# One block of a hybrid encoder: GLA's output and Hyena's second inverse transform computed by rows, Hyena's gates turned by VectorE, the last query projection by rows

## The chip, the cores and the metric

The kernel runs on one core of one Trainium2 chip. The metric is the device time of one execution in microseconds; the time of a kernel is the median of several runs. A core has TensorE (PE in the profile, with its weight loads shown apart as PEld), VectorE (DVE), ScalarE (ACT), GpSimd (POOL) and SyncE (SP), each with its own instruction queue, worked off in order; here SP issues the loads of weights and inputs, and POOL the transfers that pass a result through DRAM and back.

## The reference, cut to what matters

The kernel computes one block on 256 rows of width 2048 in f32: four mixers side by side, cross attention over 256 memory rows, a gated MLP, and a last norm.

```python
h = rms_norm(x, norm_g[l, 0])
q, k, v, g, lr, u_f, u_h, u_s = jnp.split(h @ w_in[l], split_at, axis=-1)
y_a = gla_mixer(q, k, v, g, lr, ...)                       # 512 wide
y_b = rms_norm(fnet_mixer(u_f), grp_norm_g[l, 0])          # 512 wide
y_c = rms_norm(hyena_mixer(u_h, hy_conv_w[l], filt, ...), grp_norm_g[l, 1])
y_d = rms_norm(shortconv_mixer(u_s, sc_conv_w[l]), grp_norm_g[l, 2])
x = x + jnp.concatenate([y_a, y_b, y_c, y_d], axis=-1) @ w_out[l]
x = x + cross_attention(rms_norm(x, norm_g[l, 1]), mem_n, w_q, w_kv, w_o)
x = x + swiglu(rms_norm(x, norm_g[l, 2]), w_gate_up, w_down)

# gla_mixer: 4 heads, chunks of 64 rows, forward and backward
o = rms_norm(o_intra + o_inter, norm_g) * silu(g)          # norm over the 128 of a head
# hyena_mixer: u after a convolution of three taps is split into v, x1, x2
z = x1 * long_conv(v, filt[0], skip[0])
return x2 * long_conv(z, filt[1], skip[1])                 # long_conv: rfft, product, irfft
```

## The kernel before, in words

**Layouts.** A tile *by columns* has 128 features on the partitions and the 256 rows along the free axis; a tile *by rows* has 128 rows on the partitions and up to 512 features along the free axis. A matmul reads its left operand with the contracted features on the partitions, so every result that feeds the next matrix must end by columns.

**Splitting.** f32 products are made from two fp32r parts: a high part (a cast on ACT) and a low part (a subtraction on DVE). An activation lies in a slot of 512 columns, high then low. The weights come as slabs of 1 MB; each half slab (eight blocks of 128 x 128) is cast by L102 on ACT and subtracted by L103 on DVE, a few halves ahead of its use (`Stream._half`, `Stream.take`).

**The two forms of a large product.** `gemm` (L296, L297) takes a weight block as the left operand and gives columns: per block one matmul of 512 and one of 256 columns. `gemm_rows` (L345 to L347) takes the activation as the left operand and four weight blocks as the moving one and gives rows: three matmuls of 512 columns for each half of the rows. `ROWS` lists which of the 4032 weight blocks are used by rows; it sets the place of the split tiles. What comes by rows and is needed by columns is transposed in blocks of 32 x 32 by DVE and written to DRAM (`store_turned`, L386 and L388) and read back (`load_turned`, L393), the features in a permuted order that the host puts into the weight matrix that follows (`turned`).

**Background work.** The mixers and the attention heads are Python generators. `Background.poll` is called after each weight block or pair of matmuls and lets a generator step when its due time in counted TensorE time is past and the counted DVE work owed is under 0.9 us. `yield` with a number sets the next due time; `drain` runs a generator to its end at once. `keep_place` pins instructions to their place in their engine's order.

**The part around the change**, in order of time in the profile:

- 193 to 265 us: `gemm` of Hyena's 12 column blocks. `Hyena.feed` convolves each by three taps (`conv3`); blocks 0 to 3 (v) and 4 to 7 (x1) are turned to rows by TensorE transposes (L1064) one block later, x1 is copied by ACT (L1073); blocks 8 to 11 (x2) stay by columns.
- Beside it and after it `Hyena.convs` runs: a transform (L1103), the product with the filter, an inverse transform by rows (L1103), times x1, a transform again, the product, and the second inverse transform by columns in plain f32 (L1277: 16 matmuls, each of which shows as two records), times x2. `group_norm` then sums squares by matmuls with a column of ones (L244), spreads the scale by two matmuls with a matrix of ones (L280), scales and splits into `act[16:20]`.
- 265 to 342 us: projections by rows of GLA's v, q and k, and of FNet. Then everything pending is drained, and Hyena's memory is given to GLA.
- 342 to 426 us: three projections by rows (two for the short convolution, one for GLA's gate). Beside them FNet and GLA: the gates' logarithms and running sums, the scores of each chunk (L1397, L1398), the gain of each chunk's state (`gain`, L1420, a contraction over 64 rows), the state recursion on DVE, and the output by columns (L1444, L1447), 423 to 433 us.
- GLA's output is normed over a head's 128 features, which lie on the partitions: eight matmuls with a column of ones (L244, 16 records), `rstd_end` with two matmuls of ones per head (L280), the product with the norm, then with the gate, which had been through DRAM to come by columns, and the split into `act[4:8]`.
- 426 to 453 us: the last projection of the short convolution, by columns.
- From 453 us: `out_proj` takes the 16 slots in four parts of four: Hyena, FNet, GLA, short convolution. Before each part after the first, `ready` drains the generator that fills it and loads 512 columns of x into the freed tiles through SP.
- 542 to 640 us: the query projections of the four heads; the first three by rows and through DRAM, the last one (610 to 640 us) by `gemm`, merged and split by `put` without leaving the chip. `scores` runs the heads one after another; what is left of them is drained before the last quarter of the next projection's first two column blocks (686.65 us).

## Time and profile before

| | |
|---|---|
| median of 3 runs | 1469.69 us (1469.57 to 1469.91) |
| the profiled execution | 1470.08 us |
| its span, first to last instruction | 1468.3 us |
| TensorE busy | 1458.3 us |
| VectorE, ScalarE, GpSimd busy | 921.9, 740.4, 192.1 us |
| granted TensorE clock, mean | 0.998 |

The chain rows read "start, duration, engine, tile, line", a duration being what the step adds to the chain. In timeline rows a matmul's duration runs to its modelled end and overlaps the next one, so distances between starts are what counts there. A row of waits is "who, line <- for whom: total, times, longest". In a row of windows each engine has its busy time and its instructions.

### The profile page before, as it was taken

What the parts mean: (1) busy time and instruction counts of PE and PEld (TensorE: products, weight loads), DVE (VectorE), ACT (ScalarE), POOL (GpSimd) and SP (SyncE); (2) the same over time, 40 slices, a digit from 0 to 9 for tenths busy, and PEclk for the clock granted to TensorE, in tenths of its full rate; (3) what the DMA queues carried; (4) which work ended last, traced back from release to release, by engine and by line L of the source; (5) the groups of instructions that cost most, each with busy time, mean ns of one, the idle gap of its engine ahead of it and who ended that gap; (6) DMA issues with size and microseconds to landing.
All of it is one profiled execution on the core that took longest, in us unless ns stands there. A gap on an engine that the chain in (4) does not pass through costs nothing.

```text
span 1468.3 us, 18130 instructions
## 1 busy us (share of the span) xinstructions
PE 1458.3 (99%) x6792; PEld 1214.9 (83%) x6792; DVE 921.9 (63%) x1320; ACT 740.4 (50%) x1060; POOL 192.1 (13%) x256
## 2 busy tenths in 40 slices
PE   9999999999999999999999999999999999999997
PEld 7888888888888888888888888888888888888886
DVE  6677868777778676675665555455555456444445
ACT  6566655446656455564554444444444445434344
POOL 0000000022121233520511110111110011000000
PEclk9999999999999999999999999999999999999999
DMA  9887554456556788954866666666666666555554
GB/s 348 298 282 249 207 193 168 152 202 201 198 183 211 236 265 263 267 162 151 266 219 221 225 216 198 220 226 229 214 211 216 218 211 223 198 185 190 198 200 144
DMA packets 59240, 318.07 MB, mean 217 GB/s; under 512 B 9197, under 2 KB 10894, under 8 KB 27536
## 3 DMA queue, kind: packets, MB, share of 16 engines
q1 hardware_dynamic: 46208, 281.11, 55.6%
q0 software_dynamic: 12512, 35.14, 8.9%
q8 instruction: 53, 0.87, 0.2%
q10 hardware_dynamic: 432, 0.66, 0.1%
q14 instruction: 35, 0.29, 0.1%
HBM read 297.48 MB, written 19.40 MB: 216 GB/s over the span
## 4 chain that ended last, share of the span: by engine, by line
PE 96%; ACT 1%; DVE 1%; DMA 1%; issue 0%; SPq 0%; ACTq 0%
PE pg L345 27%; PE pg L346 27%; PE pg L347 27%; PE pg L296 5%; PE pg L297 3%; PE pm L347 1%; PE pm L346 1%; PE pm L345 1%; PE pm L1103 1%; PE pm L860 1%; PE pm L831 1%; DMA raw<-in_W 0%; DVE wl L103 0%; DMA tmp<-in_cfn 0%; ACT wh L102 0%
## 5 line engine op out<-in xcount | busy, mean ns | idle before, releaser
L103 DVE TENSOR_TENSOR wl<-raw,wh 128x1024 fp32r<-128x1024 f32 (+1 forms) x503 | 611.5, 1217 | 479.3 <-ACT wh L102 478.8
L102 ACT CAST wh<-raw 128x1024 fp32r<-128x1024 f32 (+1 forms) x503 | 523.7, 1043 | 591.3 <-PE pg L347 515.3
L345 PE MATMUL pg<-wh,act 128*128 128x512 f32 (+1 forms) x1618 | 631.8, 391 | 0.4 <-ACT wh L102 0.4
L346 PE MATMUL pg<-wl,act 128*128 128x512 f32 (+1 forms) x1618 | 629.9, 389 | 0.8 <-DVE wl L103 0.8
L347 PE MATMUL pg<-wh,act 128*128 128x512 f32 (+1 forms) x1618 | 630.0, 389 | 0.0
L345 PEld LDWEIGHTS pg<-wh,act 128*128 128x128 f32 x1618 | 303.8, 188 | 64.9 <-issue 1.2
L346 PEld LDWEIGHTS pg<-wl,act 128*128 128x128 f32 x1618 | 303.9, 188 | 63.8 <-DVE wl L103 1.8
L347 PEld LDWEIGHTS pg<-wh,act 128*128 128x128 f32 x1618 | 303.8, 188 | 63.4
L296 PE MATMUL pg<-act,wh 128*128 128x512 f32 x320 | 113.0, 395 | 0.0
L297 PE MATMUL pg<-act,wl 128*128 128x256 f32 x320 | 89.8, 280 | 0.0
L296 PEld LDWEIGHTS pg<-act,wh 128*128 128x128 f32 x320 | 60.2, 188 | 12.6
L388 POOL DMA_DIRECT2D hidden<-u x22 | 16.7, 762 | 377.8 <-DVE u L386 377.8
L297 PEld LDWEIGHTS pg<-act,wl 128*128 128x128 f32 x320 | 60.2, 188 | 0.2
L347 PE MATMUL pg<-wh,f 128*128 128x512 f32 x120 | 46.8, 390 | 0.0
L345 PE MATMUL pg<-wh,f 128*128 128x512 f32 x120 | 46.8, 390 | 0.0
L346 PE MATMUL pg<-wl,f 128*128 128x512 f32 x120 | 46.7, 389 | 0.0
L393 POOL DMA_DIRECT2D tmp<-hidden x44 | 38.8, 888 | 47.3 <-DMA hidden<-u 34.6
L388 POOL DMA_DIRECT2D features<-tmp x32 | 22.7, 716 | 99.3 <-DVE tmp L386 99.3
L347 PEld LDWEIGHTS pg<-wh,f 128*128 128x128 f32 x120 | 22.5, 188 | 4.8
L346 PEld LDWEIGHTS pg<-wl,f 128*128 128x128 f32 x120 | 22.5, 188 | 4.6
L345 PEld LDWEIGHTS pg<-wh,f 128*128 128x128 f32 x120 | 22.5, 188 | 4.5
L393 POOL DMA_DIRECT2D ar<-features x24 | 21.1, 887 | 20.3 <-DMA features<-tmp 16.9
(308 smaller groups left out, 1120.6 us busy)
## 6 DMA issues: line engine op xcount, KB each, us to landing
raw<-in_W SPq DMA_DIRECT2D x246, 1024.0 KB, 5.0
raw<-in_W SPq DMA_DIRECT2D x11, 512.0 KB, 7.2
hidden<-u POOLq DMA_DIRECT2D x22, 256.0 KB, 3.5
tmp<-hidden POOLq DMA_DIRECT2D x44, 128.0 KB, 4.6
features<-tmp POOLq DMA_DIRECT2D x32, 128.0 KB, 2.3
ar<-features POOLq DMA_DIRECT2D x24, 128.0 KB, 6.3
k<-in_mem SPq DMA_DIRECT2D x8, 256.0 KB, 7.9
keys<-k POOLq DMA_DIRECT2D x8, 256.0 KB, 7.0
```

Source lines behind the costliest of these rows:

```text
L102: nc.scalar.copy(wh[:, a:b], r[:, a:b])
L103: nc.vector.tensor_tensor(out=wl[:, a:b], in0=r[:, a:b], in1=wh[:, a:b].bitcast(F32), op=ALU.subtract)
L296: self.nc.tensor.matmul(p[:, :], wh, slot[:, :], start=start, stop=False)
L297: self.nc.tensor.matmul(p[:, 0:R], wl, slot[:, 0:R], start=False, stop=stop)
L345: self.nc.tensor.matmul(p, hi, wh, start=start, stop=False)
L346: self.nc.tensor.matmul(p, hi, wl, start=False, stop=False)
L347: self.nc.tensor.matmul(p, lo, wh, start=False, stop=stop)
L388: self.nc.gpsimd.dma_start(to[r], u.rearrange("p (k c) -> p k c", c=P))
L393: self.nc.gpsimd.dma_start(t.rearrange("p (g t) -> p g t", t=32), src)
L831: nc.tensor.matmul(p[:, :], q[d][:, r * P:(r + 1) * P], kt[d][:, :], start=d == 0, stop=False)
L860: nc.tensor.matmul(p[:, 0:R], v[m][:, s], pt[m][:, c:c + R], start=m == 0 and v is vh and c == 0, stop=m == 1 and v is vl)
L1103: self.b.nc.tensor.matmul(p, a, b, start=start and n == 0, stop=stop and n == 2)
```

## The change

GLA's output matmuls swap their operands: the left one is now the scores (128 columns) or the query of one chunk (64 columns, one chunk to partitions 0 to 63 of the result and the other to 64 to 127), the moving one v or the state. The result comes by rows; the norm's sums come from ACT's accumulated squares and its scale from `rstd_cols` (DVE alone), and norm and gate are one DVE instruction per head and half of the rows. The gate stays by rows and no longer passes through DRAM; the gated output does, and is split when it has arrived and the last projection of the mixers is done. The two gains that use different halves of the partitions are issued in turns.

Hyena's second inverse transform takes the form of the first (`back`). x1 and x2 are transposed by DVE and sent through DRAM by two loads each (`turn`). The result is normed by rows, stored and loaded into `res[1]`, and split from there by `long_conv`, a background generator after GLA's start. `out_proj` takes the short convolution third and GLA fourth. The last query projection is done like the other three.

```diff
-ROWS = ((0, 512), (704, 1088), (1152, 1600), (1664, NBLK))
+ROWS = ((0, 512), (704, 1088), (1152, NBLK))
...
+                g_long = self.bg.add(self.long_conv())
...
-                for r, j in halves:
-                    t = self.tmp()
-                    nc.scalar.activation(t, ps[r][:, j:j + R], AF.Silu)
-                    self.store_turned(self.gf, j // P, r, self.tmp(), t)
-                for k in range(4):
-                    self.load_turned(gl.gate[k], self.gf, k)
+                for g, p in zip(gl.gate, ps):
+                    nc.scalar.activation(g, p, AF.Silu)
+                gl.gated = True
...
+                self.bg.drain(g_long)
                 self.gemm("w_in", [US + i * P for i in range(4)], h, ev_s)
                 gl.done = True
-                return self.out_proj(lambda n: self.bg.drain((g_fn, g_gla, g_sc)[n]))
+                return self.out_proj(lambda n: self.bg.drain((g_fn, g_sc, g_gla)[n]))
+
+    def long_conv(self):
+        nat = lambda x: x.rearrange("p (i two) -> p two i", two=2)
+        yield 14
+        for k in range(4):
+            x = self.res[1][:, k, :].rearrange("p (two i) -> p two i", two=2)
+            hi, lo = (nat(self.act[16 + k][:, c:c + R]) for c in (0, R))
+            g = self.gvec(V_GRP + 4, k)
+            mark = self.mark()
+            self.nc.scalar.activation(hi, x, AF.Copy, scale=g)
+            self.stt(lo, x, g, hi.bitcast(F32), ALU.mult, ALU.subtract)
+            self.keep_place(mark)
+            yield SOON
...
-                for c in ((0,), (2, 3), (1,))[n - 1]:
+                for c in ((0,), (1,), (2, 3))[n - 1]:
...
-        return self.gemm_rows("w_out", [0, 512], self.mix, parts=[range(k, k + 4) for k in (8, 4, 0, 12)], before=ready)
+        return self.gemm_rows("w_out", [0, 512], self.mix, parts=[range(k, k + 4) for k in (8, 4, 12, 0)], before=ready)
...
-            self.gemm("w_xq", [1536 + i * P for i in range(4)], h2, lambda i, p: last.append(self.merge(p)))
-            self.bg.add(scores(3), go=True)
+            queries(3, self.gemm_rows("w_xq", [1536], h2)[0])
...
+    def turn(self, y, d, to, j):
+        u = b.tmp()
+        b.bg.dve(R, 2)
+        for par, x in enumerate(y.rearrange("p (f b two) -> p two b f", b=4, two=2)[:, i] for i in range(2)):
+            nc.vector.transpose(u[:, par * P:(par + 1) * P].rearrange("p (b f) -> p b f", b=4), x)
+        nc.gpsimd.dma_start(d.rearrange("(t p) c -> p t c", p=P), u.rearrange("p (t c) -> p t c", c=P))
+        for par in range(2):
+            nc.gpsimd.dma_start(to[:, par, j * P:(j + 1) * P]..., d[par * P:(par + 1) * P]...)
...
-        for j in range(4):
-            for par in range(2):
-                for cs in range(2):
-                    nc.tensor.matmul(p[:, par * P:(par + 1) * P], self.y[cs][par][:, s], self.table(cs, par), ...)
-        yield from b.group_norm(out, 1, b.act[16:20])
+        yield from self.back(ps)
+        for par, x in enumerate(rows):
+            b.tt(x, ps[par], self.x2[:, par, :], ALU.mult)
+            nc.scalar.activation(ps[par], x, AF.Square, accum_out=col[:, par:par + 1])
+            yield SOON
+        yield
+        y = b.rstd_cols(col, 512)
+        for par, x in enumerate(rows):
+            nc.scalar.activation(x, x, AF.Copy, scale=y[:, par:par + 1])
+            yield
+            for j in range(0, 512, R):
+                b.store_turned(b.hf, j // P, par, b.tmp(), x[:, j:j + R])
+        for k in range(4):
+            b.load_turned(b.res[1][:, k, :], b.hf, k)
...
+        def gains(*cs):
+            us = [b.bank() for _ in cs]
+            for h in range(4):
+                for u, c in zip(us, cs):
+                    d = slice((c % 2) * 64, (c % 2) * 64 + 64)
+                    nc.tensor.matmul(u[:, h * P:(h + 1) * P], self.kr[d, c // 2, h, :], self.v[c // 2][d, h * P:(h + 1) * P], ...)
...
+        for r in range(2):
+            p = b.bank()
+            for h, hv in enumerate(heads):
+                nc.tensor.matmul(p[:, hv], self.s[r][:, h, :], self.v[r][:, hv], start=True, stop=False)
+                for i in range(2):
+                    d = slice(i * 64, i * 64 + 64)
+                    nc.tensor.matmul(p[d, hv], qs[:, h, r * P + i * 64:r * P + i * 64 + 64], st[:, 2 * r + i, h, :], start=False, stop=True)
+            for h, hv in enumerate(heads):
+                nc.scalar.activation(self.q[:, h, 0:P], p[:, hv], AF.Square, accum_out=col[:, 4 * r + h:4 * r + h + 1])
+            nc.scalar.copy(self.o[r], p)
+            yield
+        yield
+        y = b.rstd_cols(col, P)
+        while not self.gated:
+            yield
+        for r in range(2):
+            for h, hv in enumerate(heads):
+                b.stt(self.o[r][:, hv], self.o[r][:, hv], y[:, 4 * r + h:4 * r + h + 1], self.gate[r][:, hv], ALU.mult, ALU.mult)
+            ...
+                b.store_turned(b.gf, j // P, r, b.tmp(), self.o[r][:, j:j + R])
+        yield from b.arrive(b.gf, 0, b.tmp, lambda h, t: b.split_scaled(slots[h], t, b.gvec(V_GLA, 0)), 13.0, lambda: self.done)
```

122 lines of the change are left out of this document (44 added, 78 removed).

## The prediction

> **What bounds the kernel now.** I read the page's busy times first, then its chain of waits by engine, then what TensorE itself waited for.
>
> ```profile
> PE 1458.3 (99%) x6792; PEld 1214.9 (83%) x6792; DVE 921.9 (63%) x1320; ACT 740.4 (50%) x1060; POOL 192.1 (13%) x256
> ...
> PE 96%; ACT 1%; DVE 1%; DMA 1%; issue 0%; SPq 0%; ACTq 0%
> ```
> ```profile
> PE pg L346 <- DVE wl L103: 0.8, 3, 0.3
> ```
>
> TensorE is busy for 99% of the span, 96% of the chain is its instructions, and what it waits for longest once its work has begun is the low part of a weight split, 0.8 us in all. So a matmul that goes is worth its whole step in the chain, one that comes costs it, and work of DVE, ACT, POOL and SP is free until it makes a weight split or a slot late. I price the matmuls from the chain, whose durations are distances between starts, and then look for the places where the cover is thin.
>
> ```profile
> 230.38 0.23 PE pm L1064 x2
> ...
> 236.16 0.23 PE pm L1064 x2
> ...
> 242.17 0.37 PE pm L1064 x2
> ...
> 248.10 0.36 PE pm L1064 x2
> ...
> 271.08 1.37 PE pm L1103 x6
> ...
> 310.73 1.78 PE pm L1277 x16
> ...
> 315.27 1.78 PE pm L1277 x16
> ...
> 325.93 0.34 PE pm L244 x4
> ...
> 334.55 0.24 PE pm L280 x2
> ```
> ```profile
> 266.27 1.86 PE pm L469 x32
> ...
> 389.07 0.23 PE pg L347
> 389.29 0.30 PE pm L1397
> ...
> 389.60 0.11 PE pm L1397
> ...
> 390.38 0.43 PE pg L345
> ...
> 405.76 3.09 PE pm L1420 x32
> ...
> 424.04 0.39 PE pm L1447 x4
> 424.43 0.28 PE pm L1444 x2
> ...
> 438.45 1.68 PE pm L244 x16
> 440.13 0.34 PE pg L296
> ...
> 452.38 0.47 PE pm L280 x4
> ...
> 462.74 0.47 PE pm L280 x4
> ```
>
> **The change part by part: TensorE.**
>
> *x1's transposes.* The last four L1064 rows are x1's eight transposes; they go: 0.23 + 0.23 + 0.37 + 0.36 = 1.19 us gained.
>
> *Second inverse transform.* Two L1277 rows go (3.56 us), two sets of six matmuls like the L1103 row come (2 x 1.37 = 2.74): 0.82 gained.
>
> *Hyena's norm.* L244 (0.34) and L280 (0.24) go. A first large matmul behind an L244 takes 0.34 (row at 440.13) instead of 0.23, so 0.11 goes too: 0.69 gained.
>
> *GLA's norm.* L244 1.68, again 0.11 behind it, L280 twice 0.47: 2.73 gained.
>
> *The gains in turns.* The model is L1397 and L1398, two matmuls on different halves of the partitions issued in turns: the row 389.29 to the row 390.38 is 1.09 us for 16 records of each kind but only eight steps of 0.11, as the other half runs abreast. The gains' 32 records (3.09 us today) become 16 such steps, eight more than there: 1.09 + 8 x 0.11 = 1.97. Gained: 1.12.
>
> *GLA's output.* The part that can cost. Today one head and half of the rows take 0.28 (L1444) + 0.39 (L1447, four records of 64 columns) = 0.67; eight of them make 5.36. In the new form the first product keeps its shape (0.22, two records at L1397's 0.11), and the two chunks become two matmuls of 128 columns on 64 columns of the array each. Two things of that shape are not in the trace. Whether the two run abreast: the nearest row is L469, on a quarter of the array's columns, 32 records of 256 columns in 1.86 us; at L1277's 0.11 us for 128 columns they would take 7 us one behind the other, so four run abreast. I take two abreast: 0.22 for the pair, against 0.44 in series. And what changing the shape costs: the first L1397 takes 0.30 instead of 0.11, and the large matmul behind the last L1398 takes 0.43 instead of 0.23, so about 0.20 for each change. The new loop alternates full and half shape for every head and half of the rows, 16 changes. With both: 8 x (0.22 + 0.20 + 0.22 + 0.20) = 6.72, a loss of 1.36. Free changes would give 8 x 0.44 = 3.52, a gain of 1.84; paid changes with the pair in series 8.48, a loss of 3.12. I take the middle one: both its halves have a row.
> The Trainium skill, page "TensorEngine Tiling (Array Packing)", section "Key Properties", states that a change of tiling mode, as opposed to a change of tile, drains the engine, and that different tiles work independently. By it alternating at this grain speaks against the change; the 0.20 us at both ends of L1397 agree, and that section gives no price.
>
> *Last query projection by rows.*
>
> ```profile
> 254.67 0.39 PE L296 MATMUL pg<-act,wh 128*128 128x512 f32 x1
> ...
> 264.38 0.39 PE L296 MATMUL pg<-act,wh 128*128 128x512 f32 x1
> ```
> ```profile
> 290.17 0.39 PE L345 MATMUL pg<-wh,act 128*128 128x512 f32 x1
> ...
> 297.65 0.39 PE L345 MATMUL pg<-wh,act 128*128 128x512 f32 x1
> ```
>
> By columns 28 blocks take 264.38 - 254.67 = 9.71, that is 0.347 each; by rows eleven steps of three matmuls take 297.65 - 290.17 = 7.48, 0.68 a step, and two steps do four blocks, so 0.340 a block. 64 blocks: 0.43 gained.
>
> Sum on TensorE: 1.19 + 0.82 + 0.69 + 2.73 + 1.12 + 0.43 - 1.36 = **5.6 us gained**.
>
> **The change part by part: what must stay hidden.**
>
> ```profile
> 230.00:260.00 30.00, 30.00 (x176) 26.28 (x175) 29.09 (x45) 17.61 (x28) 0.00 (x0) 1.00 0.49 165
> ```
> ```profile
> L198 DVE TENSOR_TENSOR k<-k,k 128x512 f32<-128x512 f32 x24 | 16.4, 685 | 0.3
> ...
> L202 DVE SCALAR_TENSOR_TENSOR rc<-rc 128x2 f32<-128x2 f32 x36 | 5.8, 160 | 1.0
> ...
> L202 DVE SCALAR_TENSOR_TENSOR act<-tmp,vec,act 128x256 fp32r<-128x256 f32 x8 | 3.8, 479 | 0.0
> ...
> L386 DVE STREAM_TRANSPOSE tmp<-tmp 128x256 f32<-128x256 f32 x8 | 3.2, 426 | 2.2 <-ACT tmp L593 2.2
> ```
> ```profile
> 318.20 0.99 POOL L1315 MEMSET gs<- 128x512 f32 x2 [122.63 <-DVE res L198]
> ```
> ```profile
> 368.98 0.22 ACT L1384 ACTIVATE gref<-gref 128x16 f32<-128x16 f32 x1 [4.52 <-DVE gref L1362]
> ```
> ```profile
> 376.13 0.50 PE L346 MATMUL pg<-wl,act 128*128 128x512 f32 x1 [0.32 <-DVE wl L103]
> ```
>
> *Turning x1 and x2.* Sixteen half transposes on DVE, two for each of eight column blocks; a whole one of this size takes 0.43, so each pair between 0.43 and 0.86: 3.4 to 6.9 us, in a stretch where DVE is already busy for 29.09 of 30 us (the fourth pair of numbers in the window's row). They are not throttled, but Hyena's transforms beside them are: their generator steps only when little DVE work is owed. So it is the transforms that move, by about as much. Today the last Hyena matmul is at 334.55, and the drain comes with the end of FNet's projection at 342; the new chain's last matmul is the second inverse transform, today at 315.27, with the splits of its operands some 320 (an estimate: four subtractions of 0.685 on DVE). Cost 0 on TensorE. The 24 DMAs on POOL fall into the 122.63 us that it idles before 318. If that cover went, the wait is for x1, first needed behind the L1103 row at 271.08, over 20 us after the transpose of its last block at 248.10.
>
> *Hyena's result through DRAM.* Four stores and four loads on POOL, behind GLA's loads; the slots are first read by `out_proj`, four projections later. Cost 0.
>
> *`long_conv`.* This is the thin place. ACT stands 4.52 us in front of L1384 until DVE has finished GLA's running sums, its weight casts stand behind it, and the row at 376.13 shows the one stall of TensorE away from the start. Four ACT scalings and four DVE instructions of 0.48 (the second L202 row), 1.9 us on DVE, come due 14 us after 342, just ahead of it. In front of L1384 each microsecond of them is one of TensorE; in the gaps of DVE before it they are free. So 0 to 1.9, and I take 0.8: some find gaps, as the generators share the budget of owed work.
>
> *GLA's gate and output.* The gate's eight DMAs go, the output's eight come, all on POOL, which stands idle there; the split waits for the end of the mixers' last projection as before. In fourth place in `out_proj` it has a part more than now. Cost 0.
>
> *Short convolution third instead of fourth.*
>
> ```profile
> 475.75 0.24 PE pm L280 x2
> ```
> ```profile
> 479.16 1.42 DVE L198 TENSOR_TENSOR act<-res,act 128x256 fp32r<-128x256 f32 x4
> ```
>
> The third part began right behind that L280, at 476.0; the convolution's first slot was ready at 479.16 + 0.36 = 479.5. Unmoved, it would hold TensorE for 3.5 us. But GLA's norm and splits, which stood before it on DVE and in the owed budget, are mostly gone from this stretch. From 0 to 3.5 us; I take 0.4. The loads of x change places with it on SP, that of column 1 now a part earlier, the others a part later; their first reader comes after the whole product: 0.
>
> *Head 3.* Its queries now take the way through DRAM, due 18 us of counted time after the projection's end; its scores also wait for head 2 and for the values, as now.
>
> ```profile
> 682.67 1.41 PE pm L860 x12
> ```
> ```profile
> 686.65 0.39 PE L345 MATMUL pg<-wh,act 128*128 128x512 f32 x1
> ```
>
> Its last matmuls end at 684.1, and the part that needs its slots starts at 686.65. 0 to 2 us; I take 0.1, since the wait for the queries ends before the one for the values. On POOL the four stores and four loads stand in front of the last loads of values; with five buffers in use these are asked for early.
>
> **Sum.** 5.6 gained, 0.8 + 0.4 + 0.1 lost: 4.3 us. The profiled execution took 1470.08, so 1465.8; the median of the runs is 0.39 below that execution, so **1465.4 us**.
>
> **The rivals.**
>
> *Changes of shape are free at this grain.* For it: L1447 behind L1444 shows no gap, though there the shape is the same. Against: both ends of L1397 and L1420. Another 3.2 us gained: 1462.2.
>
> *The half-array pair runs in series.* For it: the two have one head's accumulator in one bank. Against: L469's four quarters share a bank too. 1.76 lost: 1467.2.
>
> *The short convolution is late in its new place*, at nearly today's pace: about 3.1 beyond my 0.4, 1468.5.
>
> *Slower: Hyena's end falls behind the drain at 342.* If the turned x1 and x2 push the transforms so far that the second inverse transform and all behind it are drained there, DVE gets, ahead of GLA's sums: four subtractions and two products of 512 columns (six by the first DVE row's 0.685: 4.1), the norm's twelve small ones (by 0.16: 1.9), four transposes (by 0.426: 1.7) and `long_conv`'s 1.9: 9.6 us, in a stretch where a late microsecond is one of TensorE. 9.6 - 5.6 = 4.0 slower than the median, 1473.7. It decides only when the chain slips by over 22 us (320 to 342); the transposes explain at most 6.9. Less of a slip brings part of it, and up to 8.5 us of stall the kernel is not over 0.2% slower.
>
> **How the numbers follow.** 0.2% (2.9 us) is about what a measurement of this kernel can tell from no change; faster is below 1466.75. My forecast 0.56, with its own range 1463.7 to 1466.7; free changes 0.09 (faster); pair in series 0.09 and late convolution 0.09 (both within); Hyena behind the drain 0.08 (slower). What I have not seen gets 0.09: 0.05 on the faster side, 0.04 on the slower. Faster 0.70, within 0.18, slower 0.12. The range 1462.0 to 1470.0 takes in free changes at its lower end, the pair in series and the late convolution, and a stall of 1.9 for `long_conv` on top of either; it leaves out the slow cases.
>
> **What the changed profile would show.** TensorE still at 99%, no L244 and L280 for Hyena and GLA. The gains near 2.0 us. GLA's output as eight groups with starts 0.8 us apart, near 0.65 if changes are free or 1.06 if the pair is in series. TensorE's waits for weight splits around 365 to 380 at 0.5 to 2 us; a DVE or ACT wait of a first matmul on the third part of `out_proj` would be the late convolution, and an L1103 behind 335 the slow case. The forecast is wrong if the waits of TensorE grow by over 3 us, wherever that is.

## The result and the profile after

The changed kernel takes 1473.46 us, the median of 13 runs (1470.85 to 1475.69), beside 1470.02 us for the kernel before: a ratio of 1.0022 (95% interval 1.0015 to 1.0029). It is slower by 0.22%; 1465.4 was predicted, with a range that ended at 1470.0. The profiled execution took 1471.93 us with a span of 1470.1, so it is one of the quicker ones.

The page's busy times and the shares of the chain by engine, after:

```profile
PE 1455.8 (99%) x6702; PEld 1207.3 (82%) x6702; DVE 924.8 (63%) x1325; ACT 737.4 (50%) x1051; POOL 222.7 (15%) x296
...
PE 96%; DVE 1%; ACT 1%; DMA 1%; issue 0%; SPq 0%; ACTq 0%; DVEq 0%
```

TensorE works 2.5 us less than before (1455.8 against 1458.3), yet the span is 1.8 us longer: the idle time of TensorE rose by 4.3 us. (0.84 us of the longer span lies ahead of the change, in the loads of the start.) Its waits (who, line <- for whom: total, times, longest), after:

```profile
PE pg L345 <- ACT act L206: 2.8, 1, 2.8
PE pm L431 <- DVE eps L432: 1.1, 1, 1.1
PE pg L346 <- DVE wl L103: 0.9, 3, 0.4
PE pm L1529 <- DVE fal L198: 0.9, 1, 0.9
PE pm L1529 <- ACT fah L214: 0.8, 1, 0.8
```

Before, the longest of these was the second kind, at the start, and the next 0.8 in all. Three are new: one of 2.8 us on a slot, and two on FNet's operand (`fah`, `fal`). The chain of after at the places whose rows the prediction priced (start, duration, engine, tile, line):

```profile
323.94 1.37 PE pm L1120 x6
328.07 1.37 PE pm L1120 x6
...
418.15 1.98 PE pm L1446 x32
...
432.59 0.37 PE pm L1474 x4
432.96 0.42 PE pm L1471 x2
433.38 0.37 PE pm L1474 x4
```

The second inverse transform is two rows of 1.37, the gains take 1.98, and GLA's output repeats every 0.79 us (432.59 to 433.38). So the work came out as it was priced. What went wrong shows when the time is cut at the first matmul of each projection. This table is worked out from both traces (durations before; differences in the profiled executions of the other kernels; e1 to e14 are told below):

```
stage                        before   after     e1     e2     e4     e6    e13    e14
Hyena's projection            71.57   -1.25  -1.25  -1.24  -1.24  +0.00  -1.24  -1.24
the next three                77.43   -1.54  -1.54  -1.54  -1.54  -0.00  -1.53  -1.54
w_in 4640 (FNet, GLA)         30.05   +0.31  +5.87  +2.75  -3.10  -0.05  -1.04  -3.44
w_in 1024                     29.05   -2.39  -2.39  -2.39  -0.90  +0.00  -2.40  -0.90
w_in 3616 by columns          27.46   +1.27  +1.28  +1.27  +1.28  -0.00  +1.27  -0.80
out_proj, first part          12.31   -1.08  +0.06  -1.07  -1.05  +0.00  -1.04  -1.04
  second part (to 3rd's start) 11.17  +4.07  +0.00  +0.61  +4.07  +1.66  +4.06  +0.61
  third part                  10.91   +1.73  +0.01  +0.36  +1.65  +0.10  +3.00  +0.28
last query projection and xo  76.65   -0.18  -0.12  -0.11  -0.15  +0.05  -0.10  -0.18
```

Every other stage differs by less than 0.05 us, but for the first 24 us, where the loads of the start vary by up to 2.0 us. Two stretches took back what the rest gained: the turn from the second to the third part of `out_proj` (+5.8), and the projection under which FNet's and GLA's chains run, which varies from +5.87 in e1 to +0.31 in the changed kernel although the instructions are the same up to there. TensorE's timeline at the third part, after:

```profile
473.32 0.28 PE L280 MATMUL pm<-dgh,ones 128*128 128x256 f32 x1
473.59 0.39 PE L280 MATMUL pm<-dgl,ones 128*128 128x256 f32 x1
476.76 0.58 PE L345 MATMUL pg<-wh,act 128*128 128x512 f32 x1 [2.79 <-ACT act L206]
477.14 0.63 PE L346 MATMUL pg<-wl,act 128*128 128x512 f32 x1
477.57 0.63 PE L345 MATMUL pg<-wh,act 128*128 128x512 f32 x1
478.00 0.63 PE L346 MATMUL pg<-wl,act 128*128 128x512 f32 x1
478.42 1.06 PE L347 MATMUL pg<-wh,act 128*128 128x512 f32 x2
479.27 0.63 PE L345 MATMUL pg<-wh,act 128*128 128x512 f32 x1
479.70 0.63 PE L346 MATMUL pg<-wl,act 128*128 128x512 f32 x1
480.13 0.55 PE L347 MATMUL pg<-wh,act 128*128 128x512 f32 x1
480.52 0.40 PE L345 MATMUL pg<-wh,act 128*128 128x512 f32 x1
```

The short convolution's first slot comes 2.79 us late, and then the matmuls start 0.427 us apart instead of 0.227 until 480.5: half speed for 3.7 us, some 1.7 us more; that is the +1.73 of the third part's row in the table. The page's clock row (9 in each of 40 slices) doesn't show it. What stood in front of the slot, on DVE and on ACT, after:

```profile
474.65 1.23 DVE L103 TENSOR_TENSOR wl<-raw,wh 128x1024 fp32r<-128x1024 f32 x1 [1.11 <-ACT wh L102]
475.79 1.27 DVE L202 SCALAR_TENSOR_TENSOR res<-res,vec,rs 128x256 f32<-128x256 f32 x3
```
```profile
474.52 0.37 ACT L283 COPY rs<-pm 128x256 f32<-128x256 f32 x1
476.31 1.20 ACT L206 CAST act<-res 128x256 fp32r<-128x256 f32 x3 [1.41 <-DVE res L202]
```

The norm's broadcast, a weight split that happens to be in between, the product and the cast follow one another, with TensorE behind them all. In the 20 us before (454 to 474), DVE is busy for 13.4 us and ACT for 9.6: they had room. So I take it that the convolution's generator came late; e1 tests this.

### The profile page after: what moved, and what is told of

The parts are those of the page before. It is cut to its first block, busy times and chain, and to the rows that moved or that the text cites. A ratio compares the mean times of both kernels' runs of the same rounds, so it can differ in the third digit from the quotient of the medians.

```text
span 1470.1 us, 18016 instructions
## 1 busy us (share of the span) xinstructions
PE 1455.8 (99%) x6702; PEld 1207.3 (82%) x6702; DVE 924.8 (63%) x1325; ACT 737.4 (50%) x1051; POOL 222.7 (15%) x296
## 4 chain that ended last, share of the span: by engine, by line
PE 96%; DVE 1%; ACT 1%; DMA 1%; issue 0%; SPq 0%; ACTq 0%; DVEq 0%
PE pg L345 27%; PE pg L346 27%; PE pg L347 27%; PE pg L296 4%; PE pg L297 2%; PE pm L345 1%; PE pm L346 1%; PE pm L347 1%; PE pm L1120 1%; PE pm L868 1%; DMA raw<-in_W 1%; DVE wl L103 1%; PE pm L839 1%; DMA tmp<-in_cfn 0%; ACT wh L102 0%
## 5 line engine op out<-in xcount | busy, mean ns | idle before, releaser
L345 PE MATMUL pg<-wh,act 128*128 128x512 f32 (+1 forms) x1650 | 645.6, 391 | 2.9 <-ACT act L206 2.8
L346 PE MATMUL pg<-wl,act 128*128 128x512 f32 (+1 forms) x1650 | 643.8, 390 | 0.9 <-DVE wl L103 0.9
L347 PE MATMUL pg<-wh,act 128*128 128x512 f32 (+1 forms) x1650 | 643.5, 390 | 0.0
L345 PEld LDWEIGHTS pg<-wh,act 128*128 128x128 f32 x1650 | 310.6, 188 | 69.4 <-ACT act L206 3.0
L346 PEld LDWEIGHTS pg<-wl,act 128*128 128x128 f32 x1650 | 310.5, 188 | 65.1 <-DVE wl L103 2.0
L347 PEld LDWEIGHTS pg<-wh,act 128*128 128x128 f32 x1650 | 310.5, 188 | 64.6
L296 PE MATMUL pg<-act,wh 128*128 128x512 f32 x256 | 89.9, 394 | 0.0
L297 PE MATMUL pg<-act,wl 128*128 128x256 f32 x256 | 71.7, 280 | 0.0
L296 PEld LDWEIGHTS pg<-act,wh 128*128 128x128 f32 x256 | 48.1, 188 | 10.6 <-issue 0.3
L297 PEld LDWEIGHTS pg<-act,wl 128*128 128x128 f32 x256 | 48.1, 188 | 0.2
```

Source lines behind the costliest of these rows:

```text
L296: self.nc.tensor.matmul(p[:, :], wh, slot[:, :], start=start, stop=False)
L297: self.nc.tensor.matmul(p[:, 0:R], wl, slot[:, 0:R], start=False, stop=stop)
L345: self.nc.tensor.matmul(p, hi, wh, start=start, stop=False)
L346: self.nc.tensor.matmul(p, hi, wl, start=False, stop=False)
L347: self.nc.tensor.matmul(p, lo, wh, start=False, stop=stop)
```

## The experiments

Theory A: the loss is the short convolution's slot, late in its new third place, and the half-speed steps that its wait sets off. Rival B: FNet's waits and GLA's changes of shape. Rival C: the slow steps have nothing to do with the wait. All medians stand beside 1470.2 to 1470.6 for the kernel before on the same chip.

**e1: the convolution's generator first in the queue.**

```diff
-                g_sc = self.bg.add(short_conv(u0), go=True)
+                g_sc = self.bg.add(short_conv(u0), first=0, go=True)
```

> The changed kernel with one word moved: the short convolution's generator is put at the head of the background queue, so that it steps before FNet's and GLA's when little work is owed. The order of the parts of `out_proj` stays as in the changed kernel. Theory A (the loss is the short convolution's slot being late at the third part, 2.79 us of wait on the split's cast, and the matmuls behind it that step 0.427 us instead of 0.227, some 1.8 us): the wait and the slow steps go together, GLA's generator is pushed back and its first slot may come up to 1 us late in the fourth part; 1473.5 - 4.6 + 0 to 1.0 = 1468.9 to 1469.9 us. Rival B (the loss is GLA's output on arrays of changing shape and FNet's waits at 374 us): the time stays within 1 us of 1473.5. Rival C (the slow steps are a thing of that place or of the chip, not of the wait): the wait goes, but eight or so matmuls still step 0.427 us near 477 us; 1470.5 or above.

1468.07 us (ratio 0.9985, 0.9975 to 0.9996), 5.4 less than the changed kernel. The wait and the slow steps at the third part are gone (+0.00 and +0.01 in the table), so A holds for this place. But the 12 runs fall into two groups, six at 1465.0 to 1466.4 and six at 1469.7 to 1472.1, and the profiled one (1471.77) shows why, at FNet (TensorE's timeline, e1):

```profile
376.40 0.73 PE L1529 MATMUL pm<-fah,fch 128*128 128x512 f32 x1 [2.11 <-ACT fah L214]
377.78 0.80 PE L1529 MATMUL pm<-fal,fch 128*128 128x512 f32 x1 [0.65 <-DVE fal L198]
378.37 0.63 PE L1529 MATMUL pm<-fah,fcl 128*128 128x512 f32 x1
...
380.08 0.63 PE L345 MATMUL pg<-wh,act 128*128 128x512 f32 x1
```

The waits that were 0.8 and 0.9 in the changed kernel's profile are 2.1 and 0.65 here, with eleven steps at half speed behind them. So a part of rival B holds too, and half speed is not tied to `out_proj`, which speaks against C. The granted clock of the runs fits this: 0.998 or 0.999 in all six quick ones, 0.996 or 0.997 in five of the six others.

**e2: the order of `out_proj` undone.**

```diff
-                return self.out_proj(lambda n: self.bg.drain((g_fn, g_sc, g_gla)[n]))
+                return self.out_proj(lambda n: self.bg.drain((g_fn, g_gla, g_sc)[n]))
...
-                for c in ((0,), (1,), (2, 3))[n - 1]:
+                for c in ((0,), (2, 3), (1,))[n - 1]:
...
-        parts=[range(k, k + 4) for k in (8, 4, 12, 0)]
+        parts=[range(k, k + 4) for k in (8, 4, 0, 12)]
```

> The changed kernel with the order of `out_proj` undone alone: GLA third, the short convolution fourth, and the loads of x as before. Theory A: the short convolution has a part more (10.9 us) and is in time; GLA's arrival is due 13 us of counted time after its store and comes to be drained at the third part, so its first scaled cast and subtraction (0.53 and 0.48 us by the changed kernel's rows) stand in front of TensorE: a wait of about 1 us there, and none of 2.8. 1473.5 - 4.6 + 1.0 = 1469.9 us, 1469 to 1471. Rival B: within 1 us of 1473.5. Rival D (GLA is what is late, whatever the order: what the third part waits for is DVE's and ACT's work, not the place in the queue): a wait of 2 us or more on GLA's slot, and 1473 to 1475 us.

1468.70 us (0.9987, 0.9979 to 0.9996): 4.8 less, a little more than A expects, and the wait for GLA's slot that I expected in its place is not there. D falls. FNet's two waits are in this profile too, 1.7 and 0.9 us, with seven steps at half speed behind them.

**e3: four changes of shape instead of sixteen.**

```diff
             for h, hv in enumerate(heads):
-                nc.tensor.matmul(p[:, hv], self.s[r][:, h, :], self.v[r][:, hv], start=True, stop=False)
+                nc.tensor.matmul(p[:, hv], self.s[r][:, h, :], self.v[r][:, hv], start=h == 0, stop=False)
+            for h, hv in enumerate(heads):
                 for i in range(2):
```

> The changed kernel, with GLA's output in two passes for each half of the rows: the four products of all 128 columns first, then the eight of 64 columns, so four changes of shape instead of sixteen; the number of matmuls and the result are the same. If a change of shape costs its 0.16 to 0.20 us each (6.08 us measured for the output against 8 x 0.44 = 3.52 with free changes), the output takes 3.52 + 4 x 0.16 = 4.2 us and the kernel 1.9 us less: 1471.6 us. If the time lies in something else (the two matmuls of a pair do not quite run abreast, or the sums into the same bank wait for each other), the output stays near 6 us and the time near 1473.5. The late short convolution is untouched: its wait of about 2.8 us stays.

1469.90 us (0.9999, 0.9990 to 1.0008), 3.6 less. The chain, e3:

```profile
431.84 0.89 PE pm L1471 x8
432.73 1.02 PE pm L1475 x16
```

Half of the output takes 1.91 us instead of 2.95 (432.37 to 435.32 in the changed kernel). The stage (`w_in` 3616) is 2.08 us shorter than in the changed kernel: 0.17 for each of the 12 changes that went. The other 1.5 us of the medians is not the shapes: in this profile FNet's first wait is 0.2 instead of 0.8.

**e4: FNet's second product due 2 us later.**

```diff
-                yield 4.0 if g else LAG
+                yield 6.0 if g else LAG
```

> The changed kernel with FNet's second product due 6.0 instead of 4.0 us of counted time behind the split of its operand, so that the cast (ACT) and the subtraction (DVE), which stand behind GLA's sums at 374 us, are done when TensorE comes to them. If the two waits at 374.40 and 375.78 (0.77 and 0.88 us) are a price of their own: they go, and the time is 1.7 us less, 1471.8 us. If the place only moves them (GLA's chain holds ACT as long, and what is behind is late instead): the waits turn up at the next product or at a weight split, and the time stays within 0.5 us of 1473.5. The late short convolution stays as it is.

1470.00 us (0.9999, 0.9991 to 1.0008), 3.5 less; ten of the 11 runs lie between 1469.0 and 1471.4. FNet's waits are gone, the convolution's (2.7) is still there. The two stages under FNet are 1.9 us shorter than in the changed kernel's quick profile; that the median gained more would fit longer waits in its slower runs, of which there is no trace.

**e5: stalls put into the kernel before.**

```diff
+        def stall(hd):
+            def done(k):
+                (start_x if hd == 3 else rows.append)(k)
+                if k in (3, 11):
+                    s = h[k + 1][:, 0:R]
+                    p = self.bank()[:, 0:R]
+                    nc.tensor.matmul(p, self.identr, s, start=True, stop=True)
+                    for _ in range((0, 9, 2, 7, 4, 5, 3, 6)[2 * hd + k // 8]):
+                        nc.scalar.copy(self.tmp(), p)
+                    nc.scalar.copy(s, p)
+            return done
...
-                    for r, p in enumerate(self.gemm_rows("w_xkv", [D + hd * 512], h, start_x if hd == 3 else rows.append)[0]):
+                    for r, p in enumerate(self.gemm_rows("w_xkv", [D + hd * 512], h, stall(hd))[0]):
```

> The kernel before with eight stalls of TensorE put into a stretch where it is otherwise never idle (the four value projections of memory, 87 us): in the middle of a product a small matmul is sent to a spare bank, ACT copies it n times and then writes the next step's slot anew with the same values, so that TensorE waits for it. n is 0, 9, 2, 7, 4, 5, 3, 6 in this order; by the rows of ACT's copies of this size (0.30 to 0.37 us each) and some 0.5 us for the way there and back the stalls are 0.8 to 3.7 us, spaced by 11 us. Theory A (the half-speed steps behind the changed kernel's 2.79 us stall are TensorE's clock, taken back after an idle time): stalls near 2.8 us and above are followed by matmuls at 0.427 us a step for 2 to 4 us, short ones are not; where the bound lies between 0.9 and 2.8 us is open. By the Trainium skill, page 'TensorE: Matmul & The Clock Gate', the clock goes by a free-running window, so the same stall may cost nothing or a window; then the bound isn't sharp. Rival C (the slow steps belong to that place in `out_proj`, where slots of several generators are written): no slow steps here, whatever the stall. The time is 1470 plus the stalls (some 18 us) and, by A, 1.7 us for each that is followed by slow steps.

1482.34 us. The stalls were not the lengths I meant, since Hyena's filter matmuls ran in the pauses. Counted from the end of the step before, an idle time of 2.2 us at 185 us and one of 1.4 + 1.1 at 115 us were followed by some eight steps of 0.427 us; 0.6 + 0.1 at 133 us and 1.2 + 0.1 + 0.6 within 2.7 us at 158 us were not. So the slow steps come from idle time, at other places too, and C has fallen. Four cases fit a plain bound on the sum between 1.9 and 2.2 us as well as a window.

**e6: the new order alone, in the kernel before.** The edit is e2's, the other way round.

> The kernel before with the new order of `out_proj` alone (short convolution third, GLA fourth, the loads of x with them). If the move alone makes the convolution late, as the prediction bounded it from the rows of before: a wait of 2 to 3.5 us at the third part and 1.8 us of half-speed steps, 1470.0 + 3.8 to 5.3 = 1473.8 to 1475.3 us. If it is late in the changed kernel because GLA's and Hyena's new work pushes it back (its steps ran some 16 us of counted time later there), the old kernel bears the new order: under 1 us of wait, no slow steps, 1470 to 1471 us.

1472.61 us (1.0013, 1.0004 to 1.0022): between the two expectations. The profile's wait (TensorE's timeline, e6):

```profile
477.93 0.50 PE L345 MATMUL pg<-wh,act 128*128 128x512 f32 x1 [1.50 <-ACT act L206]
```

The move alone makes the slot 1.5 us late, with no slow steps; the granted clock is 0.998 or 0.999 in all its runs. The last of the convolution's squares on ACT, e6, and its four squares in the changed kernel:

```profile
457.03 0.42 ACT L526 ACTIVATE tmp<-res 128x256 f32<-128x256 f32 x1 [0.27 <-DVE res L198]
```
```profile
459.96 1.33 ACT L528 ACTIVATE tmp<-res 128x256 f32<-128x256 f32 x4
```

In the changed kernel the first of them starts at 459.96 and the last at 460.9, 3.9 us later than the last one of e6, while TensorE begins to wait 2.5 us sooner (474.0 against 476.4). Draining makes up for most of that, and the wait is 1.3 us longer.

**e7 and e8: both waits mended, then the shapes too.** e7 is e2 and e4 with GLA's result due sooner; e8 adds e3's edit.

```diff
-        yield from b.arrive(b.gf, 0, b.tmp, lambda h, t: ..., 13.0, lambda: self.done)
+        yield from b.arrive(b.gf, 0, b.tmp, lambda h, t: ..., 9.0, lambda: self.done)
```

> The changed kernel with the old order of `out_proj`, GLA's result due 9.0 instead of 13.0 us of counted time after its store, and FNet's second product due 6.0 instead of 4.0: both waits mended, the arithmetic and the matmuls as in the changed kernel. If the prediction's sum on TensorE was right (5.6 us gained, 6.2 with the output's measured 6.08 us) and the two waits are all that was lost: 1470.2 - 6.2 to 6.8 = 1463.4 to 1464.0 us, and the runs lie within 2 us of each other, since a wait of varying length and a clock window behind it made the spread. If more is lost elsewhere (Hyena's transforms, the last query projection): 1465 us or above.

> The kernel of the run before this one (old order, 9.0 and 6.0), and GLA's output in two passes with four changes of shape instead of sixteen. By the single experiment's stage (2.08 us less in the short convolution's projection): 2.0 us less than the run with both waits mended, 1461.5 to 1462.0 us, and faster than both kernels. If the passes only helped by chance of the run: the same time as without them.

e7: 1465.56 us (0.9960, 0.9948 to 0.9973; 1464.2 to 1467.2), above the expected 1463.4 to 1464.0. e8: 1462.25 us (0.9940, 0.9928 to 0.9953), 0.25 us above its range and faster than both kernels. Neither is as even as expected: in their profiled executions, the slowest of five in both, TensorE waits 1.0 to 1.1 and 0.7 us for weight splits around 371.5 and 375.4 us, in a stretch where ACT's casts of FNet's tables came late (350.94 and 350.21 us).

**e9 and e10: Hyena's loads asked for later, to clear the way for FNet's tables.**

```diff
-        for k in range(4):
-            b.load_turned(b.res[1][:, k, :], b.hf, k)
...
     def long_conv(self):
+        yield 18
+        for k in range(4):
+            self.load_turned(self.res[1][:, k, :], self.hf, k)
         yield 14
```

> The changed kernel with one thing moved: the four loads of Hyena's result from DRAM (on POOL, some 344 to 350 us) are asked for by `long_conv`, due 18 us of counted time after GLA's start, instead of by Hyena's generator. Theory E (these loads share the DMA engines with the loads of FNet's tables at that very time; in the kernel before, ACT waits 1.49 us for the tables, in the changed kernel 2.91, in others with the same instructions there 2.3 to 4.4 and 1.3 more for the next two; GLA's chain and FNet's casts behind it on ACT are late by that much, and TensorE waits for FNet at 374 us): ACT's wait for the first table comes down to 1.5 to 2, FNet's two waits on TensorE (1.7 us in the profile) go or fall under 0.5, the median falls by 1.7 to 3, to 1470.5 to 1471.8, and the spread of the runs narrows by as much; the short convolution's wait of 2.8 us and its slow steps stay. Rival: the tables are late by the weights' loads in front of them on SP's queue, not by Hyena's: ACT's wait stays at 2.3 to 4.4 us and the time at 1473.5.

> The kernel of e8 (old order, GLA due at 9.0, FNet at 6.0, four changes of shape) with Hyena's loads moved as in e9. In e8's profiled execution TensorE still waits 1.0 and 0.9 us for weight splits at 370 and 374 us, behind the same late chain. By theory E these go: 1461.4 us or a little less, the lowest of e8's runs, in all runs (1460.5 to 1462). By the rival: as e8, 1462.25, with runs up to 1465.

1473.09 and 1463.04 us: no change from the changed kernel and from e8. In e9 ACT still waits 3.87 us at the first table and 1.62 at the last. But the edit did not move the loads in time. POOL's loads of Hyena's result (POOL's timeline), after and in e9:

```profile
346.54 0.89 POOL L393 DMA_DIRECT2D res<-long  x1 [5.97 <-DMA long<-tmp]
347.70 2.63 POOL L393 DMA_DIRECT2D res<-long  x3 [0.28 <-issue]
```
```profile
345.10 0.89 POOL L393 DMA_DIRECT2D res<-long  x1 [4.20 <-DMA long<-tmp]
346.27 2.64 POOL L393 DMA_DIRECT2D res<-long  x3 [0.28 <-DMA long<-tmp]
```

The generator asks for them later, but POOL has nothing to do in between and issues them as soon as Hyena's stores have landed, in e10 as well. So e9 and e10 do not test theory E, and the other traces speak for it. The tables' loads in the DMA view of the trace, with the median time from issue to landing (last number, us), before and after:

```profile
tmp<-in_cfn SPq DMA_DIRECT2D x3, 128.0 KB, 4.9
```
```profile
tmp<-in_cfn SPq DMA_DIRECT2D x3, 128.0 KB, 6.2
```

It is 4.7 to 4.9 us in the four kernels without Hyena's way through DRAM (before, e5, e6, e12) and 5.8 to 9.4 us in the ten that have it and load the tables behind the weights, e9 and e10 among them. An experiment that holds Hyena's transfers back in time is missing.

**e11: `long_conv` at the head of the queue.**

```diff
-                g_long = self.bg.add(self.long_conv())
+                g_long = self.bg.add(self.long_conv(), first=0)
```

> The kernel of e8 with `long_conv` at the head of the background queue, so that Hyena's four scalings (ACT, 0.53 us each) and subtractions (DVE, 0.48 us each) run where the prediction put them, in front of GLA's sums and the ACT instructions that wait for them, instead of 20 to 50 us later, where the last place in the queue has let them run. The prediction's term: 0 to 1.9 us of loss, 0.8 taken. If each microsecond there is one of TensorE's: waits for weight splits at 365 to 380 us longer by up to 2 us, 1463 to 1464.5. If they find gaps: 1462.2, as e8.

1462.48 us (0.9950, 0.9937 to 0.9963), e8's time within its spread, with two of the five runs at 1466. ACT's four scalings now start at 371.8 to 378.2 us instead of after 385; that is still behind GLA's sums (ACT's instruction that waits for them is at 367.0), so the place that the prediction priced was not reached. Where they ran, the work found gaps.

**e12: a ladder of stalls.** e5's stall, after the eighth step of each of twenty projections of the MLP.

> The kernel before with twenty stalls of TensorE in the MLP's gate and up projections (850 us and later), where no other matmuls of a background generator fill them: after the eighth step of each projection a small matmul is sent to a spare bank, ACT copies it n times and rewrites the next slot with the same values. n is 2, 5, 3, 7, 4, 6, 8, 3, 5, 2, 6, 4, 7, 5, 4, 6, 3, 5, 8, 4; the stalls are some 0.9 to 3.2 us long (0.3 us a copy), 22 us apart. Theory A with a bound on the length: all stalls above one length between 1.6 and 2.1 us (what lies between the single stalls seen so far: 1.5 without, 2.07 with) are followed by 8 steps at 0.427 us, none below, and the same n always gives the same. Theory A with a free-running window: stalls of the same length have it sometimes, more often the longer they are. Time: 1470 plus 20 stalls of 2 us plus 1.7 us for each that is followed by slow steps.

1548.25 us. Two stalls of the same length (n = 5, 2.82 us in the count used below; TensorE's timeline, e12):

```profile
1004.36 0.50 PE L345 MATMUL pg<-wh,act 128*128 128x512 f32 x1 [2.66 <-ACT act L942]
1004.69 0.39 PE L346 MATMUL pg<-wl,act 128*128 128x512 f32 x1
...
1131.52 0.50 PE L345 MATMUL pg<-wh,act 128*128 128x512 f32 x1 [2.66 <-ACT act L942]
...
1132.79 0.49 PE L347 MATMUL pg<-wh,act 128*128 128x512 f32 x1
1133.07 0.63 PE L345 MATMUL pg<-wh,act 128*128 128x512 f32 x1
1133.50 0.63 PE L346 MATMUL pg<-wl,act 128*128 128x512 f32 x1
```

The first has no slow steps behind it, the second has them, and only 1.4 us after it has ended. The ends of all ten slow stretches lie whole multiples of 3.413 us apart, to 0.06 us over 410 us. With windows laid on that raster, the twenty stalls sort like this (idle time from the end of the small matmul's step to the next start):

```
idle of the stall, us            2.00  2.27  2.55  2.82  3.10  3.38  3.65
stalls; of them followed by
slow steps                       2; 0  3; 1  4; 2  4; 1  3; 2  2; 2  2; 2

largest part of the idle time that falls into one window of 3.413 us
no slow steps:  1.24 1.36 1.44 1.56 1.56 1.56 1.65 1.68 1.71 1.78
slow steps:     1.94 1.99 2.11 2.11 2.26 2.46 2.87 3.28 3.33 3.41
```

Not the length decides but how much of it falls into one window: up to 1.78 us it costs nothing beyond itself, from 1.94 us the next window runs at half speed. The 24 steps behind such a stall take 1.66 to 1.73 us over their pace, against 0.09 to 0.11 behind the others: some 1.6 us more. What a stall of 2 to 3 us costs thus depends on its phase; that this differs from run to run fits the spread of the changed kernel's runs, but was not traced. That a free-running window of 3413 ns gates the clock is what the Trainium skill states, page "TensorE: Matmul & The Clock Gate", section "What's actually happening"; the raster agrees to 0.06 us. The rule of thumb in its section "HAM oscillation — how this bites in real kernels", no idle gaps above about 3.4 us, is not strict enough: 1.94 us was enough here.

**e13 to e15: FNet's tables loaded earlier.** They land in GLA's still unused output tile instead of the common small tiles.

```diff
-            x, d = b.tmp(), self.t if i < 2 else self.c
+            x, d = spare[i // 2][:, i % 2 * R:i % 2 * R + R], self.t if i < 2 else self.c
...
-                fn.open(glp)
+                fn.open(glp, gl.o)
```

> The changed kernel with FNet's three table loads landing in GLA's still unused output tile instead of the common small tiles, which puts them on SP's queue right behind GLA's two loads (331 us) and in front of two weight loads (338 us), instead of behind these (343 us). Theory F (the tables come late because they stand behind weight loads that wait for their buffers, and then share the DMA engines with them; ACT waits for the tables with GLA's chain, FNet's casts and weight casts behind it): ACT's wait for the tables goes (2.9 us in the profile, up to 4.4 in others), GLA's chain is 2 to 4 us earlier, FNet's waits at 374 us go, the runs lie closer together, and the median falls by 1.7 to 3.5 us: 1470.0 to 1471.8 (the short convolution's wait and its window stay). Rival G (GLA's chain is late by DVE's own work, and an earlier start is eaten by DVE's weight splits): FNet's waits stay, 1473.5.

> The kernel of e8 with FNet's tables early as in e13. By theory F the waits for weight splits at 370 to 374 us, which are in the slower half of the runs of e8, e10 and e11, are gone from all: 1461 to 1462 us with all runs within 1.5 us. By rival G as e8: 1462.25, with runs up to 1465.

> The kernel of e14 with FNet's second product due at 4.0 again, as in the changed kernel. By theory F the tables were the cause, so the time is that of e14 within 0.5 us, and no wait for FNet at 374 us. If the due time is what counts (ACT is held by GLA's sums at that place anyway): the waits of 0.8 and 0.9 us are back, 1.5 us slower than e14.

SP's queue before, after, and then in e13:

```profile
345.34 1.75 SPq L1485 DMA_DIRECT2D tmp<-in_cfn  x3
```
```profile
331.52 0.42 SPq L1337 DMA_DIRECT2D gmask<-in_masks  x1
338.52 4.82 SPq L81 DMA_DIRECT2D raw<-in_W  x2
343.39 2.45 SPq L1508 DMA_DIRECT2D tmp<-in_cfn  x3
```
```profile
330.86 1.94 SPq L1508 DMA_DIRECT2D go<-in_cfn  x3
337.39 6.76 SPq L81 DMA_DIRECT2D raw<-in_W  x2
```

ACT's first cast of a table, before, after, in e1 and in e13:

```profile
350.39 0.40 ACT L214 CAST fth<-tmp 128x256 fp32r<-128x256 f32 x1 [1.49 <-DMA tmp<-in_cfn]
```
```profile
349.86 0.41 ACT L214 CAST fth<-tmp 128x256 fp32r<-128x256 f32 x1 [2.91 <-DMA tmp<-in_cfn]
```
```profile
350.35 0.41 ACT L214 CAST fth<-tmp 128x256 fp32r<-128x256 f32 x1 [4.43 <-DMA tmp<-in_cfn]
```
```profile
338.73 0.41 ACT L214 CAST fth<-go 128x256 fp32r<-128x256 f32 x1 [2.00 <-DMA go<-in_cfn]
```

e13 takes 1470.21 us (1.0000, 0.9991 to 1.0009), 3.25 less than the changed kernel, and ten of its 11 runs lie within 1.8 us. FNet's first wait is gone, of the second 0.6 us are left: theory F holds, in so far as the tables' lateness has this price. The convolution's wait cost more here than in the changed kernel's profile (+3.00 against +1.73 in the third part): counted back from the end of the slow steps, 0.6 us of it fall into the following window, and 13 steps instead of 7 run at 0.427 us. e14 takes 1461.79 us (0.9944, 0.9931 to 0.9956), its runs 1461.5 to 1462.7: 11.7 us less than the changed kernel and 0.56% less than the kernel before, the best version here. e15 takes 1462.69 (0.9950, 0.9937 to 0.9962): with early tables the due time is still worth 0.9 us, a wait of 0.6 for `fal` being left.

## Why the prediction was wrong

*The work on TensorE* came out nearly as summed. Hyena's projection is 1.25 us shorter (x1's transposes, 1.19 predicted); the next three 1.54 (transform and norm, 1.51); the gains 1.98 (1.97); GLA's output 8 x 0.79 = 6.3 (6.72), so shape changes are paid and the pair runs abreast. The last query projection and the stage behind it gained 0.18, where 0.43 and a wait of 0.1 were taken. With the waits mended and the output as it is, this makes e14's 1461.8 + 2.1 (e3's stage) = 1463.9, 6.3 below the kernel before; 5.6 was summed, 6.0 with the output's measured length.

*Short convolution third instead of fourth* is the step that failed. I bounded it by 0 to 3.5 us (3.0, had I read the start of the third part rightly: it is 476.5, not 476.0) and took 0.4, because GLA's norm and splits, which stood before it, were mostly gone from that stretch. e6 shows that the move alone makes it 1.5 us late, so the bound's reading of the old order held in part; and with the change it is not earlier but 2.8 late. What DVE no longer does in that stretch was the wrong measure: the generators step in the queue's order, and by the budget of owed work. GLA, ahead of it in the queue, takes the next free budget (e1 puts the convolution first, and its wait is gone), while TensorE comes to the third part earlier by what the stages ahead have saved. Both signs that I had named came: ACT's wait at the first matmul of the third part, and idle time of TensorE that grew by over 3 us.

*What a wait costs* was the second mistake of that step. I priced a wait at its length, also in the rival that named this very mechanism (3.1 us beyond my 0.4, 1468.5, with a chance of 0.09). A wait of 2.79 us had 1.7 us of half speed behind it, in e13 some 2.9. The stage lost 5.8 us in the profile, of which 2.8 is the wait, 1.7 the slow steps, and the rest the convolution's own small matmuls that moved into it; undoing the order gave back 4.8.

*What was not in the sum at all:* FNet. Its operand depends on table loads that stand behind two weight loads on SP. These keep TensorE's pace: before and after, SP issues the tables 3.19 us behind the end of FNet's projection (345.34 and 342.15; 343.39 and 340.20). Two things changed behind that. TensorE comes to the second product 33.4 us after that end (the wait starts at 373.6) instead of 35.9 (378.08), since FNet's generator now steps earlier: 132 instead of 141 large matmuls stand in front of it. Before, the cast had been done 1.8 us ahead (376.24); in the changed kernel's profile it ends at the same distance, and the cover is gone. Which of the counted terms moved the generator isn't shown.

The tables also take longer to land, so that their first cast is 9.1 to 11.6 us behind that end in the ten kernels counted at e9, against 8.0 to 8.2 without Hyena's way through DRAM; in e1 the cast for FNet's product follows 3 us later than in the changed kernel's profile. The prediction gave that way a cost of 0, having looked only at who reads the result. It had also put the second inverse transform at some 320 us; it came at 328, so that Hyena's stores and loads run at 337 to 355 us, beside the tables. That they are what delays the tables is what the traces speak for, but no experiment here shows it. e13 puts the price of the late tables at 3.25 us of the median, more than the 1.7 of the two waits in the profile.

*`long_conv`* cost nothing: it ran from 386 to 417 us, last in the queue, and not in front of GLA's sums. At the head of the queue it costs 0.2 us, within the spread (e11); what it would cost in front of the sums was not measured. *Hyena's end* stayed ahead of the drain, with the second inverse transform at 328, so the slower rival didn't come. So from the 1463.9 us of the work alone, 4.8 for the order, 3.25 for the tables and 0.9 for FNet's due time lead to 1472.9, within 0.6 us of the 1473.46 measured; this adds up differences of medians from several kernels, and the 4.8 and the 3.25 hold the waits and their half speed together.

## What to carry to other kernels

When TensorE is 99% busy, go through the operands of the next stages, also those that the change does not touch, and ask which of them came with only a few microseconds to spare, whether the new transfers run beside their loads, and whether counted time now puts the product that reads them earlier. A load that is asked for later in the program moves in time only if its queue has something else to wait for: look at its issue in the trace before its result is read as a test. A wait that appears in a plan of due times is mended in the queue (order, due time, an earlier load), and what it costs is more than its length as soon as about 2 us of idle time fall together.

## What the runs showed of the hardware

In a kernel that is otherwise never idle, a single idle time of 2 to 3 us can set TensorE to half speed (0.427 us for 512 columns instead of 0.227) for the next window of 3.413 us. In e12 the bound lies between 1.78 and 1.94 us of idle time inside one window of a fixed raster, and 2.0 to 3.1 us of idle time had it in 6 of 16 cases, so the same stall costs 1.6 us more or nothing beyond itself. Less is enough to stay at half speed: in e13 0.6 us and in e1 about 1 us of idle time fell into the half-speed window itself, and a second one followed (13 and 11 slow steps; two cases, which give no bound). A change between a full-width matmul and two of 64 columns on the halves of the array costs 0.17 us at each change (e3). The page's clock row shows no half-speed window, and the mean granted clock of a run only in its third digit: 0.997 to 0.999 for the kernel before, 0.988 in e12 with ten windows; in e13 0.998 in the seven quicker runs and 0.996 in the four slower ones.
